# A two-block transformer kernel: the second product of each block of scores over 128 rows instead of 64

## The chip, the cores and the metric

The kernel runs on one core of one Trainium2 chip. The metric is the device time of one execution in microseconds (us). Five engines work beside one another: TensorE (PE in the profile, with its weight loads shown apart as PEld), VectorE (DVE), ScalarE (ACT), GpSimd (POOL) and SyncE (SP, which issues most transfers).

## The reference, cut to what matters

Two blocks are computed on x of 512 positions and 1024 channels. The first has a gated feed-forward part, a mixer with chunked attention over 8 heads of 64 channels (beside a pooling branch), and a second feed-forward part. The second has a differential attention with 4 heads of two components of 64 channels, an mLSTM with 4 heads whose queries and keys have 64 channels, and a squared-ReLU feed-forward part. The change is in the products of queries with keys, each a sum over 64 channels:

```python
s = jnp.einsum('bqhd,bkhd->bhqk', qb, kb).astype(jnp.float32) * scale + bias      # chunked attention, d = 64
s = jnp.einsum('bhcqd,bhckd->bhcqk', qb, kb).astype(jnp.float32) * scale          # differential attention, d = 64
scores = jnp.einsum('bhjd,bhsd->bhjs', qc, kc) * jnp.exp(logD - m_comb[..., None])  # mLSTM, d = 64
```

## The kernel before

Every operation is recorded first and issued later. Program.note keeps an operation with its engine and an assumed cost; Program.issue plans the order of each engine by 60 sweeps of a list schedule with random noise on the ranks (one draw for each operation, rng.gauss), keeps the plan with the shortest assumed makespan, and emits the operations in order of their planned start. There are two such plans: one for the first feed-forward part with the first mixer, one for all that follows. All instructions carry line 232, where they are emitted. The assumed cost of a matrix product depends on its columns alone, not on its rows.

All large products are made in three parts: each float32 operand is split by `split` into a high part, rounded to fp32r by ACT, and a low part, the rest, by DVE. Weights come in pieces of 512 KB through three raw buffers (wraw), and ACT and DVE split them into four pairs of buffers (whi, wlo). The activations are xh and xl. All else lies in two arenas: a1f and a1r are the float32 and the fp32r words of the first plan's arena, a2f and a2r those of the second. So a matrix product whose two operands are both named a1r (or both a2r) and no weight is here a product of scores, a value product of the first mixer or a selector product.

A score over 64 channels takes two products. A head uses one half of the 128 partitions, r = 64*half to 64*half+64. `stack_q` writes the high part of the queries in that half and their low part in the other. `stack_k` writes the high part of the keys, kh, in both halves, and their low part, kl, in the half r alone. The first product runs over 128 rows, the stacked queries against kh: high times high and low times high in one. The second runs over the 64 rows of r: the high part of the queries against kl. Both are issued by `qk_mm`, for one block of 128 queries at a time, with 128 to 512 columns.

Who calls it: `soft_unit`, from `soft` in mixer1 (8 heads of 4 blocks) and from `soft` in diff_phase (4 heads of 2 components of 4 blocks); and `scores` in mlstm_phase (4 heads of 4 blocks). That is 80 second products of 64 rows. The mLSTM also has, once for each head, a selector product that spreads a row of the gates over 128 partitions: sel against rr, both tiles of 36 rows, of which rows 0 to 3 hold the high part and 32 to 35 the low part.

PE has other work between the scores: projections, pooling and output products are called in between (`proj`, `pooled`, `oA`, `rope`, `conv`, `mo`, `o2a`), and the plan mixes them in.

Of the kernel before, what the change touches and what calls it, by code (L numbers as in the profile page):

```python
# [10 lines left out]
F32R = mybir.dt.float32r  # L11
I32 = mybir.dt.int32
AF = mybir.ActivationFunctionType
ALU = mybir.AluOpType

P = 128
S = 512
# [297 lines left out]
class Kern:  # L315
# [408 lines left out]
        self.split(kh[r], kl[r], src[r], None if g is None else g[r])  # L724
        self.act(kh[o], kh[r].bitcast(F32), AF.Copy)

    def qk_mm(self, out, a, b, half):

        r = slice(64 * half, 64 * half + 64)
        if isinstance(a, tuple):  # L730
            self.mm(out, a[0], b, True, False)
            self.mm(out, a[1][r], b[r], False, True)
        else:
            self.mm(out, a, b[0], True, False)
            self.mm(out, a[r], b[1][r], False, True)


    def soft_unit(self, i, q, kh, kl, half, bias, scale, E, mneg, lsum):
        w = P * (i + 1)
        e = E[:, E_OFF[i]:E_OFF[i] + w]  # L740
        ps = self.sb.next()
        self.qk_mm(ps[:, :w], q[:, i * P:(i + 1) * P], (kh[:, :w], kl[:, :w]), half)
        self.ve.tensor_tensor_reduce(out=e, in0=ps[:, :w], in1=bias[:, S - w:], op0=ALU.add, op1=ALU.min,
                                     scale=-scale, scalar=3e38, accum_out=mneg[:, i:i + 1])
        self.act(e, e, AF.Exp, scale=-1.0, bias=mneg[:, i:i + 1], accum_out=lsum[:, i:i + 1])
# [19 lines left out]
    def mixer1(self, after):  # L765
        I = self.I
        with self.mem.scope() as T:
# [21 lines left out]
            Es = [T([P, 1280])]  # L789
            PTh, PTl = T([P, 1280], F32R), T([P, 1280], F32R)  # L790
            qs, khs, kls = ([T([P, S], F32R) for _ in range(2)] for _ in range(3))
# [14 lines left out]
            def soft(h):  # L806
                mneg, lsum, rl = cols[h % 2]
                for i in (3, 2, 1, 0):
                    self.soft_unit(i, qs[h % 2], khs[h % 2], kls[h % 2], h % 2, self.T[:, h, :], 1.0, Es[h % 2],
                                   mneg, lsum)  # L810
                    e = Es[h % 2][:, E_OFF[i]:E_OFF[i] + P * (i + 1)]
                    self.ve.reciprocal(out=rl[:, i:i + 1], in_=lsum[:, i:i + 1])
                    self.ts(e, e, rl[:, i:i + 1], ALU.mult, 1.0, ALU.mult, eng=self.po)
# [23 lines left out]
            for i in range(2):  # L837
                self.act(blk[:, 64 * i:64 * i + 64], self.hm2[:, i:i + 1].to_broadcast([P, 64]), AF.Copy)
            self.ts(gq, self.col("qn"), 0.125, ALU.mult)

            self.mmb = Rot(self.B)
            banks = [self.bank() for _ in range(NT)]
# [38 lines left out]
            oB = lambda mo: out_part("oB", mo, 4, a_x[:2])  # L881
            proj(0), pooled(3), sums(0), operands(0), operands(1)
            pooled(2), pooled(1), soft(0), pooled(0)
            self.mmb = Rot(self.B[0:2])
            proj(1), soft(1), value(0), sums(1), operands(2)
            proj(2), operands(3)
            soft(2), value(1), sums(2), operands(4), oA(0)
            soft(3), value(2), proj(3), operands(5)
            soft(4), value(3), sums(3), operands(6), oA(1), oA(2)
# [50 lines left out]
    def diff_phase(self):  # L940
        I = self.I
        with self.mem.scope() as T:
            low = self.XT[:].rearrange("p t d -> p (t d)")
            dv = low[:, 0:2048].rearrange("p (t c) -> p t c", t=NT)
            E = [T([P, 1280]), low[:, 2048:3328]]
            tri = low[:, 3328:3328 + S]
            PT = T([P, 1280])
            qs, khs, kls = ([T([P, 2, S], F32R) for _ in range(2)] for _ in range(3))
# [8 lines left out]
            mneg = [T([P, NT]) for _ in range(2)]  # L957
# [12 lines left out]
            for a in range(2):  # L970
                self.split(gs[:, :, 32 * a:32 * a + 4], gs[:, :, 64 + 32 * a:68 + 32 * a], gw[:, :, 4 * a:4 * a + 4])

            self.mmb = Rot(self.B[4:8])
            banks = self.B[:4]
            self.tgroup_k(banks, [("dv", kk) for kk in range(4)], self.xs)
# [59 lines left out]
            def soft(h):  # L1035
                k = h % 2
                for i in (3, 2, 1, 0):
                    for c in range(2):
                        self.soft_unit(i, qs[k][:, c, :], khs[k][:, c, :], kls[k][:, c, :], c, tri, 0.125,
                                       E[c], mneg[c], ls[:, :, c])  # L1040
                    w = slice(E_OFF[i], E_OFF[i] + P * (i + 1))
                    self.ve.reciprocal(out=rl[:, i, :], in_=ls[:, i, :])
                    self.tt(rl[:, i, 1:2], rl[:, i, 1:2], nlam, ALU.mult)
                    self.ts(E[0][:, w], E[0][:, w], rl[:, i, 0:1], ALU.mult, 1.0, ALU.mult, eng=self.po)
                    self.stt(E[0][:, w], E[1][:, w], rl[:, i, 1:2], E[0][:, w], ALU.mult, ALU.add)
# [19 lines left out]

            rope(1)
            soft(0), value(0), rope(2)
            soft(1), conv("mq", 0), conv("mk", 0), value(1), rope(3)
            soft(2), conv("mq", 1), conv("mk", 1), value(2)
            soft(3), value(3)  # L1070

# [44 lines left out]
    def mlstm_phase(self):  # L1116
        I = self.I
        with self.mem.scope() as T:
            mv = T([P, NT, 4, P + 1])
            th = T([P, 4, S])  # L1120
            ks_ = [[T([P, S], F32R) for _ in range(2)] for _ in range(3)]
            sel, rr = T([36, S], F32R), T([36, S], F32R)
            Dm, W = T([P, 1280]), T([P, 1280])
            fs = Rot([T([P, S]), self.acc])
            sel0 = W[:36, :S]
            gl2 = T([P, 4])
            ss, den, f4 = T([P, NT]), T([P, NT]), T([P, NT])
            self.po.dma_start(sel0, I["k_sel"])
# [3 lines left out]
            self.act(rr[0:4], self.zrow[0:4], AF.Copy)  # L1132
            self.tt(rr[32:36], self.zrow[0:4], rr[0:4].bitcast(F32), ALU.subtract)
            self.ve.memset(mv[:, :, :, P:P + 1], 1.0)

            self.mmb = Rot(self.B[0:2])
            ww = [self.W(("mv", kk), 3 - kk) for kk in range(4)]
            for t in range(NT):
                b = self.bank()
                self.tgroup(b, ww, self.xs, t)  # L1140
                self.act(mv[:, t, :, :P], b[:].rearrange("p (h c) -> p h c", h=4), AF.Copy,
                         scale=self.rcol[:, t:t + 1])
# [19 lines left out]
            def scores(h):  # L1162
                mq, kh, kl = (k[h % 2] for k in ks_)
                self.stack_q(mq, self.mq[:, h // 2, :], h % 2)
                self.stack_k(kh, kl, self.mk[:, h // 2, :], h % 2)
                self.mm(rbb, sel[:, h * P:(h + 1) * P], rr)
                for s in range(NT):
                    for t in range(s, NT):
                        o = W_OFF[s] + (t - s) * P
                        dcol = self.cT[:, s, 32 * (t - s) + h:32 * (t - s) + h + 1]  # L1170
                        self.act(Dm[:, o:o + P], rbb[:, t * P:(t + 1) * P], AF.Exp, bias=dcol)
                    dd = Dm[:, W_OFF[s]:W_OFF[s] + P]
                    self.po.affine_select(out=dd, in_=dd, pattern=[[1, P]], base=0, channel_multiplier=-1,
                                          compare_op=ALU.is_ge, fill=0.0)
                for j in range(NT):
                    w = S - j * P
                    b = self.sb.next()
                    js = slice(j * P, (j + 1) * P)
                    self.qk_mm(b[:, :w], (kh[:, js], kl[:, js]), mq[:, j * P:], h % 2)
                    sl = slice(W_OFF[j], W_OFF[j] + w)  # L1180
                    self.stt(W[:, sl], b[:, :w], 0.125 * 0.25, Dm[:, sl], ALU.mult, ALU.mult)

            def value(h):
# [26 lines left out]
                self.split(*self.xs[4 + h], f, gl2[:, h:h + 1])  # L1210

            scores(0), mo(0), mo(1), mo(2), mo(3), value(0)
            scores(1), o2a(0), o2a(1), value(1)
            scores(2), o2a(2), o2a(3), value(2)
            scores(3), value(3)
            self.y = y
# [146 lines left out]
def constants():  # L1363
    import numpy as np
    e = np.eye(P, dtype=np.float32)
    tri = np.zeros((P, S), np.float32)
    tri[:, 384:] = np.where(np.arange(P)[:, None] >= np.arange(P)[None, :], 0.0, NEG)
    hm2 = np.zeros((P, 2), np.float32)
    hm2[:64, 0] = 1.0
    hm2[64:, 1] = 1.0  # L1370
    rc = np.zeros((P, 4, 16), np.float32)
    for g in range(4):
        rc[:, g, :] = 1.0 / np.minimum(np.arange(16) + 1, 2 << g)
    inv = (np.float32(10000.0) ** (-np.arange(0, 64, 2, dtype=np.float32) / np.float32(64))).astype(np.float32)
    ang = (np.arange(S, dtype=np.float32)[:, None] * inv[None, :]).astype(np.float32)
    cos, sin = np.cos(ang).T, np.sin(ang).T
    rope = np.stack([np.concatenate([cos] * 4), np.concatenate([-sin, sin] * 2)], 1).astype(np.float32)
    sel = np.zeros((36, S), np.float32)
    sel[0:4] = sel[32:36] = np.repeat(np.eye(4, dtype=np.float32), P, 1)
    return {"k_rope": rope, "k_sel": sel, "k_rcnt": rc,  # L1380
            "k_anti": e[::-1].copy(), "k_tri": tri, "k_hm2": hm2}
# [28 lines left out]
```

## Time and profile before

| | |
|---|---|
| median of 3 runs | 1546.96 us (1546.83 to 1549.86) |
| the profiled execution | 1547.03 us, span from first to last instruction 1545.2 us |
| PE busy | 1525.7 us, 99% of the span |
| DVE busy | 824.6 us, 53% |
| ACT busy | 648.4 us, 42% |
| POOL busy | 297.7 us, 19% |
| read from HBM | 137.23 MB, 90 GB/s over the span |

A busy PE is one with a product somewhere between its start and its end. Products overlap (one of 512 columns takes 0.39 us, and the next begins 0.23 us after it), so 99% doesn't say that PE is at its peak: delays between two starts that are shorter than the end of a product don't show as idle time. They are read from the starts in the timeline. The busy shares of the other engines are means over stages that differ much: DVE is busiest in the two attention stages.

### The profile page before, as it was taken

The numbers are of one execution on the slowest core, as the hardware profiler recorded it, in microseconds if no ns is written. First come the engines' busy times: TensorE is split into PE (matmuls) and PEld (weight loads), VectorE is DVE, ScalarE is ACT, GpSimd is POOL, SyncE is SP. The second block draws the span as 40 slices with busy tenths as digits, with TensorE's granted clock in tenths as the row PEclk, the third lists the DMA queues.
The fourth block names the chain that finished last, engine by engine and source line by source line (L and its number), as shares of the span: only waits on it lengthen the run. The fifth ranks groups of instructions, "written<-read, shape, count | busy, mean of one in ns | idle before, by whom it ended". The sixth has DMA issues, their size and how long they took to land.

```text
span 1545.2 us, 18001 instructions
## 1 busy us (share of the span) xinstructions
PE 1525.7 (99%) x6931; PEld 1235.2 (80%) x6931; DVE 824.6 (53%) x1284; ACT 648.4 (42%) x1063; POOL 297.7 (19%) x290
## 2 busy tenths in 40 slices
PE   9999999999999999999999999999999999999997
PEld 7888888788877788888888887677788888888886
DVE  6443443336588884433443467998568524344345
ACT  6322232234367663312322275776555634233232
POOL 5120120212243321101200146331016000000002
PEclk9999999999999999999999999999999999999999
DMA  6333333533311133333433233121221332333321
GB/s 192 96 99 95 96 103 96 114 94 111 96 55 41 55 110 96 95 96 96 113 96 95 79 99 102 42 82 49 90 69 45 123 93 95 96 95 97 95 95 55
DMA packets 226757, 140.68 MB, mean 91 GB/s; under 512 B 5340, under 2 KB 212800, under 8 KB 226672
## 3 DMA queue, kind: packets, MB, share of 16 engines
q1 hardware_dynamic: 224832, 136.33, 30.1%
q0 software_dynamic: 1824, 3.21, 1.0%
q8 instruction: 54, 0.88, 0.2%
q14 instruction: 31, 0.25, 0.1%
q10 hardware_dynamic: 16, 0.00, 0.0%
HBM read 137.23 MB, written 2.29 MB: 90 GB/s over the span
## 4 chain that ended last, share of the span: by engine, by line
PE 92%; DVE 6%; ACT 1%; POOL 0%; issue 0%; DMA 0%; SPq 0%; DVEq 0%; POOLq 0%; ACTq 0%
PE bank L232 92%; DVE a2f L232 1%; DVE wlo L232 1%; ACT a2f L232 1%; DVE X L232 1%; DVE a2r L232 0%; DVE XT L232 0%; DVE xl L232 0%; DVE a1r L232 0%; DVE sq L232 0%; DMA XT<-x 0%; DVE cv L232 0%; POOL a2f L232 0%; DVE acc L232 0%; POOL acc L232 0%
## 5 line engine op out<-in xcount | busy, mean ns | idle before, releaser
L232 DVE TENSOR_TENSOR wlo<-wraw,whi 128x1024 fp32r<-128x1024 f32 (+2 forms) x258 | 325.2, 1262 | 417.8 <-ACT whi L232 352.9
L232 ACT ACTIVATE whi<-wraw 128x1024 fp32r<-128x1024 f32 (+2 forms) x258 | 267.5, 1039 | 518.8 <-PE bank L232 498.5
L232 PE MATMUL bank<-xl,whi 128*128 128x512 f32 (+1 forms) x1272 | 463.5, 384 | 2.5 <-DVE xl L232 2.5
L232 PE MATMUL bank<-xh,whi 128*128 128x512 f32 (+1 forms) x1272 | 462.6, 385 | 1.8 <-DVE a1r L232 1.0
L232 PE MATMUL bank<-xh,wlo 128*128 128x512 f32 (+1 forms) x1272 | 458.2, 383 | 0.0
L232 PEld LDWEIGHTS bank<-xl,whi 128*128 128x128 f32 x1272 | 239.4, 189 | 50.0 <-DVE xl L232 2.9
L232 PEld LDWEIGHTS bank<-xh,whi 128*128 128x128 f32 x1272 | 238.9, 189 | 49.7 <-issue 2.2
L232 PEld LDWEIGHTS bank<-xh,wlo 128*128 128x128 f32 x1272 | 239.1, 189 | 46.5 <-issue 1.9
L232 PE MATMUL bank<-whi,a2r 128*128 128x512 f32 (+1 forms) x528 | 155.6, 388 | 0.0
L232 PE MATMUL bank<-a1r,whi 128*128 128x512 f32 x480 | 151.2, 400 | 0.0
L232 PE MATMUL bank<-a2r,whi 128*128 128x512 f32 x416 | 130.0, 397 | 0.0
L232 POOL TENSOR_TENSOR a1f<-a1f 128x512 f32<-128x512 f32 x40 | 59.5, 1487 | 317.1 <-DVE a1f L232 311.6
L232 PEld LDWEIGHTS bank<-whi,a2r 128*128 128x128 f32 x528 | 98.2, 188 | 21.0
L232 POOL TENSOR_TENSOR a2f<-a2f 128x512 f32<-128x512 f32 x38 | 56.4, 1484 | 303.5 <-DVE a2f L232 252.3
L232 PEld LDWEIGHTS bank<-a1r,whi 128*128 128x128 f32 x480 | 89.7, 188 | 22.1 <-issue 0.9
L232 PE MATMUL bank<-wlo,a2r 128*128 128x512 f32 (+1 forms) x264 | 95.0, 389 | 0.0
L232 PEld LDWEIGHTS bank<-a2r,whi 128*128 128x128 f32 x416 | 77.3, 187 | 19.0 <-issue 0.7
L232 PE MATMUL bank<-a1r,wlo 128*128 128x512 f32 x240 | 91.1, 399 | 0.0
L232 ACT ACTIVATE a2r<-a2f 128x512 fp32r<-128x512 f32 (+3 forms) x83 | 51.0, 620 | 93.3 <-POOL a2f L232 55.3
L232 DVE TENSOR_TENSOR a2r<-a2f,a2r 128x512 fp32r<-128x512 f32 (+2 forms) x81 | 54.8, 680 | 49.7 <-ACT a2r L232 48.9
L232 PE MATMUL bank<-a2r,wlo 128*128 128x512 f32 x208 | 79.4, 397 | 0.0
L232 POOL TENSOR_TENSOR X<-X,a2f 128x512 f32<-128x512 f32 (+1 forms) x9 | 10.7, 1210 | 337.6 <-ACT a2f L232 337.6
(246 smaller groups left out, 1586.0 us busy)
## 6 DMA issues: line engine op xcount, KB each, us to landing
wraw<-ffn_w_gate SPq DMA_DIRECT2D x43, 512.0 KB, 3.8
wraw<-ffn_w_up SPq DMA_DIRECT2D x43, 512.0 KB, 3.8
wraw<-w_in SPq DMA_DIRECT2D x40, 512.0 KB, 3.9
wraw<-ffn_w_down SPq DMA_DIRECT2D x32, 512.0 KB, 3.9
wraw<-w_up SPq DMA_DIRECT2D x32, 512.0 KB, 4.0
wraw<-w_down SPq DMA_DIRECT2D x32, 512.0 KB, 3.6
wraw<-w_out SPq DMA_DIRECT2D x16, 512.0 KB, 3.5
wraw<-ffn_w_down SPq DMA_DIRECT2D x16, 384.0 KB, 3.4
```

What stands on the lines that cost most here:

```text
L232: op.fn(*op.a, **op.k)
```

## The change

`qk_mm` loses its argument `half`, and its second product runs over all 128 rows. For that the half of kl that `stack_k` doesn't write has to hold zeros: `zero_half` writes them once for each kl buffer, by a copy with scale 0 on ACT. There are eight such copies of 64x512: two in mixer1, four in diff_phase (two buffers of two components), two in mlstm_phase. The selector's tiles sel and rr get 128 rows, the constant k_sel that is loaded for them too (256 KB in place of 72 KB), and its zeros lie in the added rows.

```diff
+    def zero_half(self, kl, half):
+        o = slice(64 - 64 * half, 128 - 64 * half)
+        self.act(kl[o], self.ident[o, 0:1].to_broadcast([64, S]), AF.Copy, scale=0.0)
...
-    def qk_mm(self, out, a, b, half):
-        r = slice(64 * half, 64 * half + 64)
+    def qk_mm(self, out, a, b):
         if isinstance(a, tuple):
             self.mm(out, a[0], b, True, False)
-            self.mm(out, a[1][r], b[r], False, True)
+            self.mm(out, a[1], b, False, True)
         else:
             self.mm(out, a, b[0], True, False)
-            self.mm(out, a[r], b[1][r], False, True)
+            self.mm(out, a, b[1], False, True)
...
             self.ts(gq, self.col("qn"), 0.125, ALU.mult)
+            for i in range(2):
+                self.zero_half(kls[i], i)
...
+            for kl in kls:
+                for c in range(2):
+                    self.zero_half(kl[:, c, :], c)
...
-            sel, rr = T([36, S], F32R), T([36, S], F32R)
+            sel, rr = T([P, S], F32R), T([P, S], F32R)
...
-            sel0 = W[:36, :S]
+            sel0 = W[:, :S]
...
             self.ve.memset(mv[:, :, :, P:P + 1], 1.0)
+            for i in range(2):
+                self.zero_half(ks_[2][i], i)
...
-    sel = np.zeros((36, S), np.float32)
+    sel = np.zeros((P, S), np.float32)
```

The eight added operations also shift the random draws of the planner, so that the order of all engines is drawn anew. Two places show what that does.

The first is ACT near the end of the second feed-forward part. Here `a2r<-ident` are the copies that write zeros (the one of 128x800 is there before too), `whi<-wraw` the splits of weights. Before:

```order
L232 ACTIVATE whi_77<-wraw_73 128x1024
L232 ACTIVATE a2r<-ident 128x800
L232 ACTIVATE a2r<-a2f 128x8x4 x2
L232 ACTIVATE whi_78<-wraw_74 128x1024
L232 ACTIVATE a2f<-a2f 128x512
L232 ACTIVATE a2r<-a2f 128x512
L232 ACTIVATE whi_75<-wraw_72 128x1024
```

The same place of the changed kernel:

```order
L232 ACTIVATE a2r<-ident 128x800
L232 ACTIVATE whi_77<-wraw_73 128x1024
L232 ACTIVATE a2r<-ident 64x512 x2
L232 ACTIVATE a2r<-a2f 128x8x4 x2
L232 ACTIVATE whi_78<-wraw_74 128x1024
L232 ACTIVATE a2f<-a2f 128x512
L232 ACTIVATE a2r<-ident 64x512 x2
L232 ACTIVATE a2r<-a2f 128x512
L232 ACTIVATE whi_75<-wraw_72 128x1024
```

The four copies of diff_phase have come in between, each pair just ahead of work that stood there already. The two of mixer1 stand in the same way in the first feed-forward part, and the two of mlstm_phase among the scores of the differential attention.

The second is PE at the last head of the mLSTM. Here `bank_64<-a2r` are products of scores (128 columns, the last block), `bank_65` and `bank_66` value products, `bank_68<-ident` the transposes of the head's result, and the products with whi_78 and wlo_82 output products of the attention (`o2a`), which fill in. Before:

```order
L232 MATMUL bank_66<-a2f 128x129 x3
L232 MATMUL bank_64<-a2r 128x128 x2
L232 MATMUL bank_61<-a2r,whi_78 128x512
L232 MATMUL bank_62<-a2r,whi_78 128x512
L232 MATMUL bank_65<-a2f 128x129 x2
L232 MATMUL bank_66<-a2f 128x129 x4
L232 MATMUL bank_68<-ident,a2f 128x128 x4
L232 MATMUL bank_62<-a2r,wlo_82 128x512
```

The same place of the changed kernel:

```order
L232 MATMUL bank_64<-a2r 128x128
L232 MATMUL bank_66<-a2f 128x129 x3
L232 MATMUL bank_64<-a2r 128x128
L232 MATMUL bank_62<-a2r,whi_78 128x512
L232 MATMUL bank_68<-ident,a2f 128x128
L232 MATMUL bank_61<-a2r,whi_78 128x512
L232 MATMUL bank_65<-a2f 128x129 x2
L232 MATMUL bank_66<-a2f 128x129 x4
L232 MATMUL bank_62<-a2r,wlo_82 128x512
L232 MATMUL bank_68<-ident,a2f 128x128 x3
```

Neighbours have changed places, and the transposes stand one or two products later; the order of the stages is the same. Behind the last transposes 15 rows of output products follow before, and 13 in the changed kernel, ahead of the products that need this head (`o2B`).

## Rows read from the trace of the kernel before

**Rows 1.** The page: busy time and share of PE.

```profile
PE 1525.7 (99%) x6931; PEld 1235.2 (80%) x6931; DVE 824.6 (53%) x1284; ACT 648.4 (42%) x1063; POOL 297.7 (19%) x290
```

**Rows 2.** The chain of waits, longest pieces: start us, us, what.

```profile
439.36 516.53 PE bank L232 x2279
...
1012.16 3.19 DVE a2f L232 x4
1018.71 145.25 PE bank L232 x743
```

**Rows 3.** Timeline around one second product of mixer1: start us, us, what.

```profile
513.52 0.40 PE L232 MATMUL bank<-a1r,wlo 128*128 128x512 f32 x1
513.85 0.18 PEld L232 LDWEIGHTS bank<-a1r 64*128 64x128 f32 x1 [0.36 <-issue]
513.85 0.49 PE L232 MATMUL bank<-a1r 64*128 64x512 f32 x1
...
514.27 0.19 PEld L232 LDWEIGHTS bank<-a1r,whi 128*128 128x128 f32 x1 [0.24 <-issue]
514.27 0.51 PE L232 MATMUL bank<-a1r,whi 128*128 128x512 f32 x1
514.37 0.19 PEld L232 LDWEIGHTS bank<-a1r,wlo 128*128 128x128 f32 x1
514.61 0.40 PE L232 MATMUL bank<-a1r,wlo 128*128 128x512 f32 x1
...
514.84 0.40 PE L232 MATMUL bank<-a1r,whi 128*128 128x512 f32 x1
```

**Rows 4.** Weight loads of 64 rows: mixer1 from 439, second half of diff_phase, whole kernel.

```profile
L232 PEld LDWEIGHTS bank<-a1r 64*128 64x128 f32 x30 | 5.5, 183 | 7.2 <-issue 6.8
...
L232 PEld LDWEIGHTS bank<-a2r 64*128 64x128 f32 x16 | 2.7, 183 | 3.8 <-issue 3.3 <-DVE a2f L232 0.4
...
L232 PEld LDWEIGHTS bank<-a2r 64*128 64x128 f32 x48 | 8.4, 183 | 12.5 <-issue 11.0 <-DVE a2f L232 0.7 <-DVE cv L232 0.4
```

**Rows 5.** Products by form, whole kernel: count | busy us, mean ns.

```profile
L232 PE MATMUL bank<-a2r 64*128 64x512 f32 x12 | 6.0, 497 | 0.0
...
L232 PE MATMUL bank<-xl,a2r 128*36 128x512 f32 x8 | 2.0, 394 | 0.0
L232 PE MATMUL bank<-a2r 36*128 36x512 f32 x4 | 2.0, 497 | 0.0
```

**Rows 6.** Timeline of PE, two second products side by side.

```profile
1007.11 0.33 PE L232 MATMUL bank<-a2r 64*128 64x128 f32 x2
```

**Rows 7.** Busy us (count) of PE, PEld, DVE, ACT, POOL in stretches; then granted clock.

```profile
439.00:560.00 121.00, 120.64 (x551) 91.36 (x552) 101.87 (x215) 83.48 (x168) 41.70 (x49) 1.00 0.19 57
955.00:1019.00 64.00, 61.70 (x280) 44.16 (x279) 57.97 (x127) 50.78 (x103) 25.66 (x22) 1.00 0.22 58
1019.00:1077.00 58.00, 58.00 (x283) 44.83 (x283) 50.06 (x135) 40.30 (x98) 12.54 (x14) 1.00 0.20 56
1077.00:1164.00 87.00, 87.00 (x464) 69.42 (x463) 51.28 (x140) 46.39 (x119) 12.96 (x24) 1.00 0.26 79
...
971.00:1009.00 38.00, 36.76 (x167) 25.81 (x166) 35.74 (x97) 30.61 (x69) 13.24 (x13) 1.00 0.10 29
50.00:400.00 350.00, 350.00 (x1531) 285.42 (x1530) 145.76 (x167) 104.78 (x128) 50.01 (x46) 1.00 0.36 100
1172.00:1176.00 4.00, 1.29 (x9) 0.88 (x7) 3.98 (x5) 2.68 (x6) 4.00 (x5) 0.92 0.46 132
1176.00:1180.00 4.00, 3.77 (x17) 3.77 (x18) 4.00 (x7) 1.43 (x3) 3.15 (x4) 0.50 0.41 120
```

**Rows 8.** An ACT copy of the zeros' shape, whole kernel: count | busy us, mean ns.

```profile
L232 ACT ACTIVATE a2r<-a2f 64x512 fp32r<-64x512 f32 x24 | 14.9, 627 | 4.4 <-POOL a2f L232 2.9 <-PE bank L232 1.2
```

**Rows 9.** Transfers on POOL's queue: KB, us from issue to landing.

```profile
XT<-k_tri POOLq DMA_DIRECT2D x1, 256.0 KB, 3.0
...
a2f<-k_sel POOLq DMA_DIRECT2D x1, 72.0 KB, 3.6
```

More of the change, by code (lines that the diff above doesn't have):

```diff
@@ L725, in stack_k, with soft_unit @@
         self.act(kh[o], kh[r].bitcast(F32), AF.Copy)
-    def qk_mm(self, out, a, b, half):
-        r = slice(64 * half, 64 * half + 64)
+    def zero_half(self, kl, half):
+        o = slice(64 - 64 * half, 128 - 64 * half)
+        self.act(kl[o], self.ident[o, 0:1].to_broadcast([64, S]), AF.Copy, scale=0.0)
+    def qk_mm(self, out, a, b):
         if isinstance(a, tuple):
             self.mm(out, a[0], b, True, False)
-            self.mm(out, a[1][r], b[r], False, True)
+            self.mm(out, a[1], b, False, True)
         else:
             self.mm(out, a, b[0], True, False)
-            self.mm(out, a[r], b[1][r], False, True)
-    def soft_unit(self, i, q, kh, kl, half, bias, scale, E, mneg, lsum):
+            self.mm(out, a, b[1], False, True)
+    def soft_unit(self, i, q, kh, kl, bias, scale, E, mneg, lsum):
         w = P * (i + 1)
@@ L741, in soft_unit @@
         ps = self.sb.next()
-        self.qk_mm(ps[:, :w], q[:, i * P:(i + 1) * P], (kh[:, :w], kl[:, :w]), half)
+        self.qk_mm(ps[:, :w], q[:, i * P:(i + 1) * P], (kh[:, :w], kl[:, :w]))
         self.ve.tensor_tensor_reduce(out=e, in0=ps[:, :w], in1=bias[:, S - w:], op0=ALU.add, op1=ALU.min,
@@ L808, in soft @@
                 for i in (3, 2, 1, 0):
-                    self.soft_unit(i, qs[h % 2], khs[h % 2], kls[h % 2], h % 2, self.T[:, h, :], 1.0, Es[h % 2],
+                    self.soft_unit(i, qs[h % 2], khs[h % 2], kls[h % 2], self.T[:, h, :], 1.0, Es[h % 2],
                                    mneg, lsum)
@@ L1038, in soft @@
                     for c in range(2):
-                        self.soft_unit(i, qs[k][:, c, :], khs[k][:, c, :], kls[k][:, c, :], c, tri, 0.125,
+                        self.soft_unit(i, qs[k][:, c, :], khs[k][:, c, :], kls[k][:, c, :], tri, 0.125,
                                        E[c], mneg[c], ls[:, :, c])
@@ L1178, in scores @@
                     js = slice(j * P, (j + 1) * P)
-                    self.qk_mm(b[:, :w], (kh[:, js], kl[:, js]), mq[:, j * P:], h % 2)
+                    self.qk_mm(b[:, :w], (kh[:, js], kl[:, js]), mq[:, j * P:])
                     sl = slice(W_OFF[j], W_OFF[j] + w)
```

## The prediction

> **What bounds the kernel now.** I read the page first: PE is busy 99% of the span [rows 1], so PE is the first suspect everywhere, and any time taken out of PE's stream counts. The chain of waits, read next, corrects this. From 439.36 us on, through mixer1's scores and the second feed-forward part, the chain is PE alone for 516.53 us, and again for 145.25 us from 1018.71 [rows 2], which covers the second half of diff_phase and the mLSTM. Between them, from about 956 to 1018.71, it runs mainly over DVE, and the reader sees one of those pieces in the rows. There PE's time is not what ends last.
>
> The busy share hides how PE spends its time, so I then read the starts in the timeline around one second product [rows 3]. A product of 512 columns normally starts 0.23 us after its predecessor (514.61 to 514.84). The 64-row product at 513.85 starts 0.33 after the one before it. The next full one starts 0.42 after that, at 514.27, and the next again 0.34 later, at 514.61. Only then is the rhythm back. So one 64-row product in a stream of 128-row ones holds PE up by 0.33 + 0.42 + 0.34 - 3 x 0.23 = **0.40 us**. The weight loads show how. The load of the 64-row product starts only with its own product, as does that of the full product behind it; both were preceded by idle time that the profile puts down to issue (0.36 and 0.24). The loads further on run ahead, beside the product before theirs (514.37). The 48 loads of 64 rows in the second plan lost 11.0 us to issue, and 30 of those in mixer1 6.8 [rows 4], and this is only the first part of each delay.
>
> Is it the rows? The selector product, 36 rows from partition 0, has the same 497 ns as the 64-row products of 512 columns, against 394 ns for a product of 128 rows and only 36 columns [rows 5]. Rows are common to the slow ones, not the half in which they lie and not the columns.
>
> **The change, part by part.** *Removed.* 48 products of 64 rows in the second plan [rows 4], 32 in mixer1 (8 heads of 4 blocks) and 4 selector products of 36 [rows 5], 84 x 0.40 = 33.6 us. They stream the same columns with 128 rows; a 128-row product of 512 columns costs 0.23 whatever its rows hold. Two second products that stood next to each other started together, at 1007.11 [rows 6], and another pair does so at the end of diff_phase's second half; each pair was delayed once, not twice, and will run one after the other, so I take 0.4 off for each: 32.8 us of PE time in all. No cost arises below nothing here: the columns stay.
>
> *What of it lies on the path.* I take the stages one by one, with the busy time of DVE as the limit, since DVE's work doesn't change [rows 7].
> - Mixer1, 439 to 560: 30 products [rows 4] (the two others lie just before 439.36, where PE isn't on the chain), 12.0 us. 121 - 12.0 = 109.0 us would have DVE busy 101.87, or 93%.
> - diff_phase, first half, 955 to 1019: 16 products (half of diff_phase's 32), 6.0 us, but DVE is on the chain there and busy 57.97 of 64, or 91%.
> - diff_phase, second half, 1019 to 1077: 16 products [rows 4], 6.0 us. 58 - 6.0 = 52.0 us would have DVE busy 50.06, or 96%.
> - mLSTM, 1077 to 1164: 16 products and 4 selectors, 8.0 us. 87 - 8.0 leaves DVE (51.28) at 65%.
>
> How full can DVE be? Where it is on the chain it reached 91% over 64 us, and 35.74 of 38, or 94%, in the densest part, 971 to 1009 [rows 7]. These are the two bounds. I take 93%, nearer to the upper one, because the 64 us include the start of the stage with its long dependencies. Mixer1 then ends after 101.87 / 0.93 = 109.5 and gains 11.5; the first half 57.97 / 0.93 = 62.3, gains 1.7; the second half 50.06 / 0.93 = 53.8, gains 4.2; the mLSTM gains all of 8.0. Sum **25.4 us**. With 94% it is 12.0 + 2.4 + 4.7 + 8.0 = 27.1, with 91% 9.1 + 0 + 3.0 + 8.0 = 20.1.
>
> *Added.* Eight copies of zeros on ACT; one is like the copy of the same shape at 627 ns [rows 8], so 5.0 us of ACT. Six stand in the feed-forward parts, where ACT is busy 104.78 of 350 us [rows 7], and are hidden by PE's stream. Two stand among the scores of diff_phase, where ACT would be busy (40.30 + 1.3) of some 54 us, or 77%. If both lay on the chain they would cost 1.3 us; I take nothing. What stands behind them on ACT are weight splits and the copies of the next head, and those have PE's other products as cover. Every second product now also reads the zeros, but these are written long before the first of them. k_sel grows to 256 KB on POOL's queue; a transfer of that size took 3.0 us, the one of 72 KB 3.6 [rows 9], so the size costs nothing to see. rr and sel are copied with the same columns.
>
> *Moved.* The whole order is drawn anew. The stages and the mix stay alike at the two places shown, so I give this nothing in the sum and some 2 us either way in the range.
>
> **A rule against the row.** One rule would change the sum. The Trainium skill, "TensorE: Matmul & The Clock Gate", Part 3, under "The mechanism", says that a weight load overlaps products in flight only when it goes to another row group. By it a 128-row load could not run beside a 128-row product, and padding would take the overlap away. The rows say the reverse: the 128-row load at 514.37 ran inside the product from 514.27 to 514.78, and the 64-row load waited [rows 3]. By the row the sum is the 32.8 us above, by the rule the fourth rival below.
>
> **The rivals.** 1. *All of it arrives.* DVE has slack that its share doesn't show, because part of its busy time can move into neighbouring stages with PE's. Then 1547 - 32.8 = 1514 us. For it speaks that mixer1 and the second half of diff_phase have PE on the chain from end to end; against it, 96% for DVE in a stage where it reached 94%.
> 2. *DVE is the bound at its present share.* If the 84% of mixer1 (101.87 of 121) and the 86% of the second half (50.06 of 58) are all that the dependencies allow, those stages give nothing, and only the mLSTM's 8.0 us remain: 1539 us. Against it: the chain there is PE, not DVE.
> 3. *The rows are not the cause*, and the delay belongs to these products' operands or their place. Then nothing changes: 1547 us. The 36-row selector speaks against it.
> 4. *The padded loads can't run ahead.* Then each product would save 0.40 but pay its own load of 0.19 [rows 3], 84 x 0.21 = 17.6 us: 1529 us. The overlapping loads speak against it.
> 5. *Slower: the new order leaves the last mLSTM head uncovered.* Its result is needed by all of o2B, and PE already ran dry there: 1.29 of 4 us busy from 1172 on, after which the granted clock was 0.50, the lower of its two levels (1.2 GHz), from 1176 to 1180 [rows 7]. If the filling products were used up earlier, PE would idle longer at that place and run at half speed longer. It decides once idle time and half clock there exceed the 25 us gained elsewhere, so that an added 30 us gives 1552. The order shows 13 rows of filling there, against 15, which is near to what it was.
>
> **How the numbers follow.** The profiled execution took 1547.03 us (span 1545.2, so 1.8 us around it), the median is 1546.96; the difference doesn't matter. Likeliest: 1547.0 - 25.4 = **1522 us**, from 1518 to 1528 by the two bounds on DVE and the new order. Chances: this 0.48, all of it 0.22, DVE at its present share 0.22, padded loads 0.03, no effect 0.03, slower 0.02. The range goes from 1512 (all of it, with 2 us from the new order) to 1533: DVE at 91% gives 1527, and half of the way from there to the second rival is 1533. A change of 0.2%, about 3 us, is what a measurement of this kernel can tell from none. Faster by more: 0.48 + 0.22 + 0.22 + 0.03 = 0.95; within it 0.03; slower 0.02.
>
> **What the new profile would show.** Right: no weight load of 64 or 36 rows except in small transposes, score products at 0.23 us from start to start, the idle time put down to issue gone from their loads, mixer1 and the mLSTM shorter by some 11 and 8 us, the first half of diff_phase nearly as long as before with DVE still on the chain, and DVE over 90% busy in both attention stages. Wrong: starts 0.33 and 0.42 apart around 128-row score products (third rival), loads waiting for the product before (fourth), DVE on the chain in mixer1 at a share under 90% (second), or a long idle PE at a low granted clock before o2B (fifth).

## The result, and the profile after

The changed kernel takes 1529.09 us (median of 4 runs, 1528.13 to 1529.82), the kernel before, on the same chip, 1548.11. The ratio is 0.9876, with a 95% interval from 0.9859 to 0.9893, so 19.0 us were gained (16.6 to 21.8), against 25.4 in the prediction's sum; the time lies within its range of 1512 to 1533 and 1 us above the narrower one, 1518 to 1528, that went with the sum. The profiled execution has a span of 1528.1 us.

The timeline of PE around one second product of mixer1 in the changed kernel, start us, us, what:

```profile
510.79 0.39 PE L232 MATMUL bank<-a1r,wlo 128*128 128x512 f32 x1
511.02 0.40 PE L232 MATMUL bank<-a1r 128*128 128x512 f32 x1
511.25 0.39 PE L232 MATMUL bank<-a1r,whi 128*128 128x512 f32 x1
511.48 0.40 PE L232 MATMUL bank<-a1r,wlo 128*128 128x512 f32 x1
```

The starts are 0.23 us apart on both sides of the score product, the second line, where [rows 3] had 0.33, 0.42 and 0.34. Its weight load runs inside the product ahead of it:

```profile
510.79 0.19 PEld L232 LDWEIGHTS bank<-a1r 128*128 128x128 f32 x1
```

The groups of weight loads of the same kernel, by form:

```profile
L232 PEld LDWEIGHTS bank<-a1r 128*128 128x128 f32 x128 | 22.5, 189 | 7.7 <-DVE a1f L232 3.8 <-DVE a1r L232 0.5 <-ACT a1r L232 0.4
...
L232 PEld LDWEIGHTS bank<-a2r 128*128 128x128 f32 x100 | 17.9, 189 | 8.2 <-DVE a2f L232 4.3 <-DVE a2r L232 1.6
```

No load of 64 or 36 rows is left, and the idle time ahead of these loads is put down to DVE and ACT, no longer to issue as in [rows 4]. The stalls are gone, then, and others have come. The page shows them as idle time of PE:

```profile
PE 1499.4 (98%) x6931; PEld 1233.2 (81%) x6931; DVE 823.4 (54%) x1284; ACT 652.0 (43%) x1071; POOL 295.6 (19%) x290
```

PE is busy 26.3 us less than in [rows 1], while the span shrank by 17.1. The chain of waits of the changed kernel, its longest pieces, says where PE stopped being the bound:

```profile
415.10 2.00 POOL a1f L232
...
442.14 15.65 PE bank L232 x73
459.96 4.80 POOL a1f L232 x4
467.31 1.87 POOL a1f L232
476.40 19.33 PE bank L232 x100
...
516.02 436.70 PE bank L232 x1938
...
1040.31 106.95 PE bank L232 x617
...
1175.76 328.30 PE bank L232 x1474
```

In [rows 2] PE's piece ran without a break from 439.36. Now mixer1 is broken up by pieces of POOL and, in the lines left out, of DVE and ACT, and PE has the chain to itself only from 516. The stages of the changed kernel (busy us and count of PE, PEld, DVE, ACT, POOL; then the granted clock):

```profile
440.00:554.00 114.00, 111.27 (x550) 89.88 (x550) 103.56 (x216) 84.08 (x168) 45.76 (x49) 1.00 0.21 65
949.00:1068.00 119.00, 111.47 (x565) 89.26 (x564) 111.06 (x262) 92.96 (x205) 37.73 (x36) 1.00 0.22 60
1068.00:1147.00 79.00, 79.00 (x463) 69.39 (x463) 50.34 (x139) 46.04 (x118) 11.62 (x24) 1.00 0.29 87
1147.00:1176.00 29.00, 25.05 (x180) 23.07 (x179) 26.84 (x45) 14.68 (x31) 19.66 (x23) 0.94 0.19 55
```

Against [rows 7] the mLSTM (third line) is 8 us shorter, and PE fills it as before. In mixer1 and the differential attention PE is idle for 2.7 and 7.5 us, against 0.4 of 121 and 2.3 of 122 in [rows 7], and DVE is busy for 91% and 93% of the time.

To see each stage by itself I compare the starts of the same pieces of work. The splits of the weights on DVE (`wlo<-wraw,whi`) come in one fixed order, 258 of them; five of them mark the stages. Before, the 73rd, 99th, 172nd, 184th and 198th start at 374.9, 571.3, 965.7, 1078.5 and 1194.3 us; in the changed kernel at 376.6, 565.5, 957.5, 1068.9 and 1177.9. Between the first two lies mixer1, between the next two the second feed-forward part, then the differential attention, then the mLSTM. Where two kernels have the same order of instructions, the second feed-forward part comes out alike to 0.1 us, which is about what this measure can tell there. Lengths in us, for all the kernels of this study:

| kernel | mixer1 | second feed-forward | differential attention | mLSTM |
|---|---|---|---|---|
| before | 196.3 | 394.4 | 112.7 | 115.8 |
| changed | 188.9 | 392.0 | 111.4 | 109.0 |
| e1, order of before, padded | 187.9 | 394.4 | 107.9 | 108.3 |
| e2, order of the changed kernel, 64 rows | 195.4 | 391.9 | 114.7 | 116.3 |
| e3a, only mixer1 padded | 188.0 | 394.4 | 112.7 | 115.8 |
| e3b, only differential attention padded | 196.4 | 394.4 | 107.9 | 115.8 |
| e3d, only the selectors padded | 197.9 | 394.4 | 112.7 | 114.3 |
| e4, less DVE work, 64 rows | 199.4 | 394.4 | 110.7 | 115.8 |
| e5, less DVE work, padded | 187.2 | 394.5 | 104.2 | 108.4 |
| e7, less POOL work, 64 rows | 196.4 | 394.4 | 112.6 | 115.8 |
| e8, less POOL work, padded | 186.4 | 394.4 | 106.0 | 108.3 |
| e9, less of both, padded | 186.0 | 394.4 | 103.3 | 108.3 |
| e6, second seed | 191.3 | 394.2 | 112.0 | 106.6 |
| e6, third seed | 191.5 | 394.0 | 109.2 | 108.1 |

### The profile page after: what moved, and what is told of

Same layout as the page of the kernel before. It is cut to its first block, busy times and chain, and to the rows that moved or that the text cites. A ratio compares the mean times of both kernels' runs of the same rounds, so it can differ in the third digit from the quotient of the medians.

```text
span 1528.1 us, 18002 instructions
## 1 busy us (share of the span) xinstructions
PE 1499.4 (98%) x6931; PEld 1233.2 (81%) x6931; DVE 823.4 (54%) x1284; ACT 652.0 (43%) x1071; POOL 295.6 (19%) x290
## 4 chain that ended last, share of the span: by engine, by line
PE 87%; DVE 8%; ACT 2%; POOL 1%; issue 1%; DMA 0%; SPq 0%; DVEq 0%; POOLq 0%; ACTq 0%
PE bank L232 87%; DVE a2f L232 2%; DVE wlo L232 1%; POOL a1f L232 1%; ACT a2f L232 1%; DVE a1f L232 1%; DVE X L232 1%; DVE a2r L232 1%; DVE sq L232 1%; DVE XT L232 1%; ACT whi L232 0%; DVE a1r L232 0%; DVE cv L232 0%; DMA XT<-x 0%; DVE xl L232 0%
## 5 line engine op out<-in xcount | busy, mean ns | idle before, releaser
L232 ACT ACTIVATE a2r<-a2f 128x512 fp32r<-128x512 f32 (+2 forms) x83 | 50.9, 619 | 89.4 <-POOL a2f L232 53.2
L232 DVE TENSOR_TENSOR a2r<-a2f,a2r 128x512 fp32r<-128x512 f32 (+3 forms) x81 | 55.8, 692 | 48.7 <-ACT a2r L232 48.0
L232 POOL TENSOR_TENSOR X<-X,a2f 128x512 f32<-128x512 f32 (+1 forms) x9 | 10.9, 1218 | 336.0 <-ACT a2f L232 336.0
```

The source lines that it names most:

```text
L232: op.fn(*op.a, **op.k)
```

## The experiments

Two questions were open: how much of the change is the padding and how much the new order, and what holds back the part of the padding's gain that didn't arrive.

**Padding and order apart.** In e1 the zero copies are left out of the planner's input (no draw of noise falls to them) and put in behind an ACT operation that stands near them in the program. All engines then have the order of before, with the eight copies added on ACT.

```diff
-        first, ops = self.first, self.ops[self.first:]
+        every = self.ops[self.first:]
+        ops = [op for op in every if op.near is None]
...
+        for op in every:
+            if op.near is not None:
+                op.start = max([op.near.start] + [p.start for p in ops if op.i in p.succ]) + 0.5
```

> The padded kernel with the order of the kernel before on every engine (the zero copies are left out of the planning and put in beside work that stands there). Theory 1, the order is neutral and DVE's work limits the gain: near the changed kernel, 1526 to 1531 us. Theory 2, the new order costs several us, part of the gain is lost to it: clearly faster than the changed kernel, 1514 to 1523 us. In both the starts around score products are 0.23 us apart.

Measured: 1526.39 us, ratio 0.9863 (0.9849 to 0.9876). The interval overlaps that of the changed kernel (0.9859 to 0.9893), and the time lies at the lower end of what theory 1 gave.

In e2 the order is that of the changed kernel to the last instruction, and only the rows that are issued differ.

```diff
             self.mm(out, a[1], b, False, True)
+            self.only(r, a[1], b)       # the recorded product gets lhsT[r], rhs[r]
...
                 self.mm(rbb, sel[:, h * P:(h + 1) * P], rr)
+                self.only(slice(0, 36), sel[:, h * P:(h + 1) * P], rr)
```

> The order of the changed kernel, zero copies included, but the second products and the selector products issued over 64 and 36 rows as before. Theory 1, the order is neutral: 1546 to 1550 us, as before. Theory 2, the new order costs several us by itself: 1552 to 1558 us.

Measured: 1545.78 us, ratio 0.9989 (0.9980 to 0.9997). With 64 rows the new order, zero copies included, costs nothing; it is 1.7 us better. Theory 2 falls in the form in which it was put. But the two orders do differ once the stalls are gone: in the old one the stages shrink by 8.4, 4.8 and 7.5 us (before to e1), in the new one by 6.5, 3.3 and 7.3 (e2 to the changed kernel). By the stages of one profile each, the order that was the better one with stalls is the worse one without: the four stages sum to 801.3 us in the changed kernel and 798.5 in e1, with 64 rows to 818.3 (e2) and 819.2 (before). The times of the whole kernels don't show it, since the intervals of their ratios overlap.

**One stage at a time**, all in the order of before.

```diff
-    self.qk_mm(ps[:, :w], q[:, i * P:(i + 1) * P], (kh[:, :w], kl[:, :w]))
+    self.qk_mm(ps[:, :w], q[:, i * P:(i + 1) * P], (kh[:, :w], kl[:, :w]), half)   # None where the stage is padded
```

> The order of before, only the second products of mixer1 over 128 rows. Theory 1: the gain of the forecast for this stage, 11.5 us, so about 1536.5 us. If POOL or the dependencies hold mixer1 as they do in the changed kernel, 7 us: 1541. If all stalls are gained, 13 us: 1535.

Measured: 1539.16 us, ratio 0.9943 (0.9929 to 0.9956), a gain of 8.8 us by the ratio. By the stage it is 8.3, all of it in mixer1. The forecast's 11.5 for this stage is refuted.

> The order of before, only the second products of the differential attention over 128 rows. Theory 1, DVE limits the stage: 6 us (1542 us), nearly all of it in the second half, DVE over 92% busy from 955 us to the end of the stage. Theory 2, DVE is no limit and the order was: all 12 us (1536 us).

Measured: 1543.07 us, ratio 0.9969 (0.9956 to 0.9981), 4.8 us by either measure, near to theory 1's 6. PE's products come in the same order as before, so the starts can be compared one by one: about 1.0 us of the gain lies in the first half and 3.8 in the second, so not nearly all in the second. DVE is busy for 108.10 of the 116 us from 955 on, or 93%, as theory 1 had it.

> The order of before, only the four selector products of the mLSTM over 128 rows in place of 36. If fewer rows than 128 are the cause of the stalls, 4 x 0.40 = 1.6 us less, all of it in the mLSTM, and the three starts behind each selector product 0.23 us apart. If the cause lies with the second products' operands, nothing.

Measured: 1545.56 us, ratio 0.9988 (0.9977 to 0.9998). The mLSTM is 1.5 us shorter, from 115.8 to 114.3. Around a selector product of this kernel the starts are in rhythm:

```profile
1080.16 0.39 PE L242 MATMUL bank<-whi,xl 128*128 128x512 f32 x1
1080.39 0.39 PE L242 MATMUL bank<-a2r 128*128 128x512 f32 x1
1080.62 0.39 PE L242 MATMUL bank<-whi,xh 128*128 128x512 f32 x1
1080.85 0.39 PE L242 MATMUL bank<-wlo,xh 128*128 128x512 f32 x1
```

Its operands are not those of the second products, and its 36 rows begin at partition 0; four of them gave about four times the stall that was read from one second product. So the rows are the cause for products of 64 and of 36 rows. The kernel's one product of 71 rows (and 71 columns, at 156.67 us before) shows no such stall: the starts around it are 0.23, 0.03, 0.32 and 0.23 us apart, some 0.1 us in all over the rhythm. Rows between 64 and 128 occur nowhere else here, so where the stall begins isn't shown.

What padding gives back depends on the columns. Over the three starts around a score product that stands alone, before against e1, it is 0.39 us for most products of 256, 384 and 512 columns, but 0.29 to 0.35 for most of 128. At 1084.33 us before, a product of 128 columns has 0.15, 0.25 and 0.34 between the starts; in e1 the same ones are 0.06, 0.11 and 0.28, not back in a rhythm of 0.23 behind it.

**What holds the rest.** The prediction had DVE as the limit in both attention stages. e4 and e5 take DVE work away, with 64 and 128 rows; e7 and e8 take POOL work away; e9 takes both. The planner still plans these operations, so that the order stays, but they are not issued; these five kernels compute something else and serve for their times alone.

```diff
                 self.tt(self.X[:, m, :], b, self.X[:, m, :], ALU.add)
+                self.prog.ops[-1].drop = key != "oC"        # e4, e5, e9; also two groups of diff_phase
...
                 self.ts(e, e, rl[:, i:i + 1], ALU.mult, 1.0, ALU.mult, eng=self.po)
+                self.prog.ops[-1].drop = True               # e7, e8, e9; also the same step of diff_phase
```

> The order of before and products of 64 rows, with DVE work left out of both attention stages: in mixer1 the 16 additions to X behind the output products of oA and oB (11.0 us of DVE), in the differential attention the 16 additions of the second component's weights and the 12 products of the convolutions (20.6 us). It is the base for the next kernel. Where PE is the bound already, hardly faster than before: 1540 to 1546 us, the difference from the first half of the differential attention.

> The same work left out, with products of 128 rows. Theory 1, DVE's busy time limits the gain: with 11.0 and 20.6 us less of it padding now gains nearly all, 12 to 13 us in mixer1 and 11 to 12 in the differential attention, against 8.2 and 4.9 with all of DVE's work. Rival, the gain is held by the chain of a head's steps through DVE, ACT and POOL, whatever their shares: 8 to 9 and 5 to 6 as before.

Measured: 1545.32 and 1522.81 us. Theory 1 fails for mixer1. Its 187.2 us in e5 are 9.1 less than before, where 8.4 came with all of DVE's work, and not 12 to 13. (The 199.4 of e4 contain 6.8 us at half clock, shown further below, so before's 196.3 is the base.) The differential attention is 2.0 us shorter in e4, and padding gains another 6.5 (110.7 to 104.2): more than the 4.8 with all of DVE's work, far less than 11 to 12.

> The order of before and products of 64 rows, with POOL's scaling of the softmax weights left out: 32 in mixer1 (20.8 us of POOL), 16 in the differential attention (11.3 us). It is the base for the next kernel; within 3 us of before if PE is the bound.

> The same work left out, with products of 128 rows. Theory 1, DVE is the limit: the gain stays at 8 to 9 us in mixer1 and 5 in the differential attention. Rival, POOL's steps in the chain of a head hold mixer1: its gain rises to 11 to 13 us, and that of the differential attention to 6 or more.

Measured: 1547.44 and 1523.11 us. With 64 rows taking POOL's steps away is worth nothing in any stage. With 128 rows padding gains 10.0 us in mixer1 (196.4 to 186.4) and 6.6 in the differential attention (112.6 to 106.0), while DVE has all of its work. POOL is busy under 40% of these stages in e1, and yet taking its steps out gives more in mixer1 than taking DVE's additions out; but it was also more work (20.8 us of POOL against 11.0 of DVE), so the two are not ranked by this. The gain is below the rival's 11 to 13, so it is not POOL alone either. In the differential attention the 6.6 meet what the rival said.

> The order of before, products of 128 rows, with both kinds of work left out of the attention stages: DVE's 11.0 and 20.6 us and POOL's 20.8 and 11.3 us of the runs before. Theory 1 in its new form, the gain is held by the chain of a head's steps that runs through DVE and POOL: the two reliefs add up, mixer1 ends 10.5 to 12 us earlier than before (8.5 with all work, 9.2 and 10.0 with one kind left out), the differential attention 9 to 12 (4.9; 8.5 and 6.5). Rival, ACT or PE's own order holds the rest: no more than with the better of the two, 10.0 and 8.5.

Measured: 1519.71 us, ratio 0.9821 (0.9801 to 0.9841). Mixer1 is 10.3 us shorter than before, between the rival's 10.0 and the band that began at 10.5, so e9 doesn't decide there whether the two reliefs add up (0.7 and 1.5 us alone, 1.9 together). The differential attention is 9.4 us shorter, inside the band and above the rival's 8.5. The stretch of mixer1's scores in e1:

```profile
439.00:552.00 113.00, 110.75 (x552) 90.61 (x553) 101.37 (x215) 83.31 (x168) 42.51 (x49) 1.00 0.20 61
```

and in e9:

```profile
439.00:552.00 113.00, 112.43 (x562) 92.91 (x563) 94.96 (x202) 85.17 (x171) 24.31 (x18) 1.00 0.20 61
```

In e9 PE is busy all but 0.6 of 113 us. In e1 DVE reached 90% here, and the chain of waits of e1 shows how it shares the bound (start us, us, what):

```profile
439.60 12.93 PE bank L242 x56
...
460.32 3.96 POOL a1f L242 x4
464.29 1.45 POOL sq L242
...
467.34 2.22 POOL a1f L242
469.58 1.21 ACT a1r L242 x2
...
473.06 0.75 DVE a1r L242
...
474.60 13.90 PE bank L242 x73
...
513.42 46.68 PE bank L242 x233
```

Here POOL scales the four blocks of one head's weights (the x4), squares and multiplies for the norm of the next heads (sq, a1f), ACT and DVE split that result into the operands of the next scores, and only then PE goes on. These steps follow one another, and with the stalls gone PE's filling work runs out before they end. PE's order is that of before to the last product, so the places can be found. The first, in e1:

```profile
473.34 0.34 PE L242 MATMUL bank<-a1r 128*128 128x384 f32 x1
474.60 0.51 PE L242 MATMUL bank<-a1r 128*128 128x256 f32 x2 [0.92 <-DVE a1f L242]
```

These two starts are 1.26 us apart, and 0.18 before. At two more places, 510.27 and 512.75 us, 0.26 and 0.24 became 0.87 and 0.67. With POOL's steps left out (e8) the three are 0.82, 0.26 and 0.28, with DVE's additions left out (e5) 1.26, 0.36 and 0.66, with both (e9) 0.82, 0.26 and 0.23. So both engines hold these places, and what is left of the first one is due to neither kind of work that was left out.

**Other orders.** The changed kernel with two other seeds.

```diff
-        rng = random.Random(1)
+        rng = random.Random(2)      # and 3
```

> The changed kernel with another seed of the planner's noise, so another order of all engines. Its measure is the spread that an order by itself makes: by the two orders that ran so far, 1526.4 and 1529.1 us, I expect 1524 to 1532.

> The changed kernel with a third seed. The same: 1524 to 1532 us.

Measured: 1532.31 us, ratio 0.9901 (0.9887 to 0.9916), just above the range, and 1531.52 us, ratio 0.9901 (0.9884 to 0.9917), inside it. Over the four orders that ran with padding the ratio goes from 0.9863 to 0.9901, some 6 us. In mixer1 the four lengths are 187.9, 188.9, 191.3 and 191.5. Of all kernels that compute everything e1 has the lowest ratio; its interval lies clear of the two seeds' and overlaps that of the changed kernel.

## Why the prediction was right, and where it was off

- *The stall of 0.40 us and its cause, the rows.* Right. The starts are in rhythm after the change, the score products' loads no longer wait for issue, and the selectors alone gave 1.5 us for four. It was read from one product of 512 columns, and taken for all: padding gave back less at products of 128 columns.
- *The mLSTM gains all of 8.0 us.* Right within 1 us: 7.5 in the old order, 7.3 in the new. DVE has 64% there, and PE stays on the chain. Most of the missing half us is that of the four blocks of 128 columns, at 0.29 to 0.35 each.
- *The differential attention gains 1.7 + 4.2.* Right in kind: far less than 12, since other engines take over. It was 4.8 in the old order (about 1.0 and 3.8 in the two halves) and 3.3 in the new.
- *Mixer1 gains 11.5.* This is the term that was mis-sized: 8.4 in the old order, 6.5 in the changed kernel. The step that failed is to take DVE's busy share as the only limit and to let it rise to 93%. Relief of DVE alone gave 0.7 us there, of POOL alone 1.5. What the runs showed in its place is a chain of a head's steps across POOL, ACT and DVE. None of them is full, and the chain was hidden before because PE's stalls kept PE later than it: with the stalls, leaving POOL's steps out gave nothing. Start by start, the padding gave back 10.9 us around the 32 score products in e1, and other starts of mixer1 moved apart by 2.4, most of it at the three places above. POOL was not looked at as a limit in the prediction.
- *The new order is worth nothing, some 2 us either way.* Right for the kernel with stalls (1.7 us better), and off for the one without: 2.0 us worse than the old order by the ratios (0.9876 and 0.9863 of 1548), though their intervals overlap, and 5.9 with the other seeds, whose intervals don't.
- *The zero copies and the larger k_sel are hidden.* e2 has both, and isn't slower than before. In the order of before, the stages that aren't padded keep their lengths with the copies and the larger constant in place: 196.4 for mixer1 in e3b, 112.7 and 115.8 for the two others in e3a, as before to 0.1 us.
- *The rivals.* All of it arriving is refuted by the idle PE in both attention stages, DVE at its present share by the 91% and 93% above and by the 8.3 us that mixer1 gained alone. Padded loads do run ahead: the starts around them are 0.23 us apart. The fourth rival, in which a 128-row load does not overlap, gave 1529 us, which is the measured time, but for another reason: by it the mLSTM, where PE is the bound, would gain 20 x 0.21 = 4.2 us, and it gained 7.5. The sentence of the Trainium skill that stood behind it ("TensorE: Matmul & The Clock Gate", Part 3, under "The mechanism": "LDWEIGHTS overlaps with in-flight MATMULs only when row_grp differs"), taken by itself, does not agree with this case's traces, where the 128-row load at 510.79 us runs inside a 128-row product. The same section of the Trainium skill also has a load pulled ahead when it goes to the background weight buffer, which the prediction left out; no run shows where a load goes. The last head of the mLSTM was not uncovered: ahead of o2B PE is busy 25.05 of 29 us at a granted clock of 0.94 (1147 to 1176, fourth line of the stages above), against 24.67 of 28 at 0.88 before (1164 to 1192).

What stays open: counted at 0.40 us each, mixer1's 32 products have 12.8 us of stalls. In e9 11.0 of that came back around them (10.9 in e1), and other starts took 0.7, which leaves the 10.3; part of the 1.8 that is missing lies in the products of 128 columns, the rest was not traced further. Nor was it tried why the new order loses 1.5 us more than the old one in the differential attention.

## What to carry to other kernels

Read the distance between starts, not the busy share: a PE that is 99% busy lost some 0.4 us at each of 84 products with 64 or 36 rows, in a stream of products of 128 rows, and zeros in the missing rows gave back 0.39 of it with 256 columns or more, and some 0.3 with 128. Then ask of each stage which chain was hidden by the stall, step by step and across all engines. Room in the busiest engine's share gives only an upper bound of the gain, and the engine that takes over may be one that is busy a third of the time. Where a planner draws the order anew, compare at one order before the gain is put down to the edit.

## What the runs showed that I had not expected

The granted clock can fall in one run and not in another at the same place. Just ahead of mixer1's scores PE is idle for about 1.2 of 4 us. In the kernel before the clock stayed at 1.00 (the higher level, 2.4 GHz):

```profile
436.00:440.00 4.00, 2.79 (x11) 1.51 (x10) 3.94 (x6) 2.15 (x3) 1.81 (x2) 1.00 0.45 131
440.00:444.00 4.00, 4.00 (x16) 2.67 (x15) 3.60 (x14) 3.12 (x9) 2.05 (x3) 1.00 0.00 0
```

In e4, with PE busy to the same hundredth of a microsecond or so, it fell to 0.50 (1.2 GHz):

```profile
436.00:440.00 4.00, 2.80 (x10) 1.67 (x9) 3.94 (x8) 1.76 (x3) 1.24 (x1) 0.92 0.44 130
440.00:444.00 4.00, 4.00 (x9) 2.36 (x8) 2.55 (x12) 2.11 (x8) 2.27 (x3) 0.50 0.00 0
```

PE started 9 products in those 4 us in place of 16, and mixer1 came out 3.1 us longer than before (199.4 against 196.3) with less work in it. A single profile of a stage that begins behind such a gap can be off by that much; e3d, with 3.4 us at 0.50 from 440.9 on, is 1.6 us longer in a mixer1 that it doesn't touch.
